# A gathered retrieval beside a dense one: table rows fetched in pairs, the dot products split over two engines, and one more block's top-k inside the dense stage

## The chip, the cores and the metric

One Trainium2 chip, one core. The metric is the time of one execution on the device in microseconds (us). The engines are TensorE (PE: matmuls; PEld: its weight loads), VectorE (DVE), ScalarE (ACT), GpSimd (POOL) and SyncE (SP), and 16 DMA engines move the data. Each engine takes its instructions in the order of its own queue.

## The reference

One decoder layer on 1024 tokens of width 1024: a modulated norm, gMLP heads and an S5 state-space part side by side, an output projection with a residual, then a retrieval over 16384 experts, and a final norm. The retrieval is what matters here:

```
q = (t @ w_q).reshape(tb, HEADS, 2, DKEY // 2)              # t: a block of 128 tokens
s = einsum('thcd,hckd->thck', q, keys)                      # 8 heads, 2 halves, 128 keys
top_s, top_i = top_k(s, 16)                                 # per half
cand = all sums of one entry of each half;  best_s, pos = top_k(cand, 16)
idx = the experts of pos;  g = softmax(best_s)
act = gelu(einsum('thkd,td->thk', u_tab[idx], t))           # first table
return einsum('thk,thkd->td', g * act, v_tab[idx])          # second table
```

So each token uses 128 expert slots (8 heads of 16), each with a row of 1024 fp32 in the first table (`peer_u`) and one in the second (`peer_v`).

## The kernel before

The tokens form 8 blocks of 128. A **lead** of some 920 us computes everything up to the scores, along a written-out plan (`CFG["plan"]`): each item, such as `r6`, which is `route(6)`, the top-k of block 6, has a due time and a number of steps, and the items' steps are put in order by those times. A planner of the framework then sets each engine's queue order from that program order and its own estimate of when operands are ready. On the chip the order of a queue is fixed.

**Dense stage, blocks 0 to 4.** Their 640 tokens meet all 16384 experts, in 128 tiles of 128 experts. For tile `i`, `stage1(i)` (L918 to L933) multiplies the tile of the first table, split into a high and a low part `uh`, `ul`, with the tokens, `Th` and `Tl`, into PSUM banks `pa`: 48 matmuls (L930), and a gelu on ScalarE (L932) frees the bank. `load_u(i + 2)` brings the tile through one buffer `ur` (ScalarE casts the high part, L906; VectorE subtracts, L907), `load_v(i)` the tile of the second table through one buffer `vr` (L914, L915). `weigh` multiplies two tiles' results by the routing weights of the group (`Gt`, L949) and splits them into `wh` and `wl` (L951, L953). After every fourth tile `stage2` multiplies the group's weights with its `v` tiles: 120 matmuls `pd` (L977) and `res` (L968); VectorE adds what `pd` gives to `acc` (L985). The first five tiles' `stage1` lies in the lead.

**Gathered blocks 5 to 7.** `side_work()` is a generator that the dense loop advances: `pull(6)` after each tile. It first runs `route(b)` for the blocks from `NDB + early` on, which is block 7 alone; its 28 steps work on VectorE, and the scores come from DRAM by SyncE's queue, two heads at a time (`scr`, L761). Then the pool `kp` of the top-k is closed and the pool `rp` opened. For each block there are 128 steps on the first table: GpSimd gathers a row per token (L872), and one fused VectorE instruction multiplies it with `hn` and sums (L875) into a column of `act`. Then 128 steps on the second table: a gather (L883) and a multiply-add into `gacc` (L888). Rows live in a ring of six. At a block's end `load_x1` (on GpSimd's queue, kept in program order) brings the tokens' residual, and `finish` (L829 to L845) multiplies by `gt2`, adds, norms and writes out. The two constant rows for `finish`, `gt2` and `g_final`, are loaded once by `final_rows`, into two tiles of their own.

**The end.** After the loop `pull(10 ** 9)` draws what is left of the generator; then the last `stage2` loads five blocks' residuals on GpSimd's queue (L851) and calls `finish` for the five dense blocks. For them VectorE multiplies and adds straight from PSUM banks (L835, L836), which is what frees those banks. The loop:

```
    for i in range(NE):
        if i >= L: run(stage1(i))
        if L <= i + 2 < NE: load_u(i + 2)
        ...
        if i % 2: weigh(i // 2)
        if i % QG: load_v(i)
        pull(cfg["per"])
        if i % QG == 0:
            ...
    pull(10 ** 9)
    stage2(NGR - 1)
```

Of the kernel before, what the change touches and what calls it, by code (L numbers as in the profile page):

```python
# [21 lines left out]
P = 128  # L22
# [14 lines left out]
NS = NH * TOPK  # L37
NE = 128
QG = 4
FMAX = 3.0e38  # L40
CFG = dict(xo=[2, 3, 4, 0, 1], gt=3, ss=7, hs=2, b1=6, nw=6, raw=1, ngb=3, rows=6, lead=5, per=6, dv=[6, 9, 9, 2, 99], early=2,
           hp=600, eo=(2, 4), em={2: 'pppxx', 4: 'Xpp'}, seg=4, plan=dict(
    op0=(-238.2, 44.5), sb0=(-21, 248.8), m5=(-490.1, 3.4), r0=(234.1, 82.1), op1=(132.1, 27.3), op2=(292.7, 7.7),
    sb1=(310, 10.8), op3=(364.9, 36.8), r1=(301.9, 79), s0=(261.5, 137.5), sb2=(303.2, 61.7), zv=(372.6, 16.7),
# [23 lines left out]
def rows(ap, n=P):  # L68
    return bass.AP(tensor=ap.tensor, offset=ap.offset, ap=[[0, n]] + [list(d) for d in ap.ap])
# [27 lines left out]
def tile_hybrid_layer(ctx: ExitStack, tc: tile.TileContext, a, out, cfg=CFG):  # L97
# [752 lines left out]
    def load_x1(b, x1):  # L850
        tc.keep_in_program_order(nc.gpsimd.dma_start(x1, x1_d[b * P:(b + 1) * P, :]))  # L851
        return x1

    def final_rows(pool):
        for n, src in enumerate((gt2_d, rows(a["g_final"]))):
            fin.append(pool.tile([P, D], F32, name=f"fin{n}", bufs=1))
            nc.scalar.dma_start(fin[n], src)

    def side_work():
        for b in range(NDB + cfg["early"], NB):  # L860
            yield from route(b)
        kp.release()
        rp = rq[0] = ctx.enter_context(tc.tile_pool(name="rp", bufs=cfg["rows"], side="left"))
        final_rows(rp)
        for n in range(NGB):
            ix, gw = tops[NDB + n]
            hn = rp.tile([P, D], F32, tag="hn", name=f"hn{n}", bufs=1)
            nc.scalar.dma_start(hn, h2_d[n * P:(n + 1) * P, :])
            act = rp.tile([P, NS], F32, tag="act", name=f"act{n}", bufs=1)
            for s in range(NS):  # L870
                row = rp.tile([P, D], F32, tag="row", name=f"ru{n}_{s}")
                G.indirect_dma_start(out=row, out_offset=None, in_=a["peer_u"],  # L872
                                     in_offset=bass.IndirectOffsetOnAxis(ap=ix[:, s:s + 1], axis=0))
                junk = rp.tile([P, D], BF16, tag="junk", name=f"jk{n}_{s}", bufs=1)
                V.tensor_tensor_reduce(out=junk, in0=row, in1=hn, scale=1.0, scalar=0.0, op0=ALU.mult,  # L875
                                       op1=ALU.add, accum_out=act[:, s:s + 1])
                yield
            A.activation(act, act, AF.Gelu_apprx_tanh)
            V.tensor_mul(act, act, gw)
            ac = rp.tile([P, D], F32, tag="hn", name=f"gacc{n}", bufs=1)  # L880
            for s in range(NS):
                row = rp.tile([P, D], F32, tag="row", name=f"rv{n}_{s}")
                G.indirect_dma_start(out=row, out_offset=None, in_=a["peer_v"],  # L883
                                     in_offset=bass.IndirectOffsetOnAxis(ap=ix[:, s:s + 1], axis=0))
                if s == 0:
                    V.tensor_scalar(ac, row, act[:, 0:1], None, op0=ALU.mult)
                else:
                    V.scalar_tensor_tensor(ac, row, act[:, s:s + 1], ac, op0=ALU.mult, op1=ALU.add)  # L888
                yield
            x1 = load_x1(NDB + n, rp.tile([P, D], F32, tag="row", name=f"xf{n}"))  # L890
            finish(NDB + n, x1, [(slice(0, D), ac)], rp, *fin)

    side = side_work()
# [1 line left out]
    def pull(n):  # L895
        for _ in range(n):
            if next(side, 0) == 0:
                return
# [196 lines left out]
    for i in range(NE):  # L1095
# [9 lines left out]
            weigh(i // 2)  # L1105
        if i % QG:
            load_v(i)
        pull(cfg["per"])
        if i % QG == 0:
            if i >= max(L, 1):  # L1110
                stage2(i // QG - 1)
# [352 lines left out]
```

## Time and profile before

| | |
|---|---|
| time, median of 3 runs | 2660.49 us (2659.53 to 2662.55) |
| profiled execution | 2662.87 us, span of its instructions 2661.1 us |
| TensorE busy | 95% |
| VectorE busy | 86% |
| ScalarE busy | 34% |
| GpSimd busy | 41% |
| DMA, mean | 272 GB/s |

The span runs from the first to the last instruction of the profiled execution; 1.8 us of its time lie around it. Times in the rows below are microseconds from the span's start unless marked ns. An engine's share is taken over the whole span, which has a lead, a dense stage and a tail with different limits. Matmuls are pipelined, so a busy TensorE is not one at its peak rate.

### The profile page before, as it was taken

The page shows a single profiled execution, that of the slowest core. Times are in us where ns is not written, and L with a number is a line of the kernel's source. Part 1 is how long each engine was busy: PE and PEld are TensorE (multiplying, and loading weights), DVE is VectorE, ACT ScalarE, POOL GpSimd, SP SyncE. Part 2 cuts the span into 40 slices and gives each one's busy share as a digit, 9 for nine tenths or more (in the row PEclk, how much of TensorE's full clock was granted, in tenths as well). Part 3 has the DMA queues.
Part 4 walks back from the last instruction along what each step waited for, and adds up shares of the span by engine and source line. Part 5 has one row for each costly group of instructions (what it writes and reads, how often), then busy time and mean ns, then how long its engine had stood idle before and what let it go on. Part 6 is the DMA issues. An engine that isn't in the chain of part 4 may idle for free.

```text
span 2661.1 us, 38843 instructions
## 1 busy us (share of the span) xinstructions
PE 2539.9 (95%) x14119; PEld 2174.0 (82%) x14119; DVE 2295.9 (86%) x4791; ACT 900.7 (34%) x1547; POOL 1093.2 (41%) x842
## 2 busy tenths in 40 slices
PE   6999999999877999999999999999999999999996
PEld 3557676678666899999999999999999999999995
DVE  7884699869899798888998888888898888888898
ACT  2211246568968322222222222222222222222221
POOL 0001000000000066566666566666666566666662
PEclk9996999999987999999999999999999999999998
DMA  9555333444646699999999999999999999999995
GB/s 366 103 151 177 109 117 105 128 135 135 172 120 191 217 359 344 344 331 336 333 349 348 317 351 336 348 345 332 334 337 345 344 337 336 340 344 345 324 322 188
DMA packets 301184, 724.74 MB, mean 272 GB/s; under 512 B 42384, under 2 KB 133008, under 8 KB 300576
## 3 DMA queue, kind: packets, MB, share of 16 engines
q0 software_dynamic: 112832, 411.09, 42.8%
q1 hardware_dynamic: 165600, 254.48, 28.8%
q10 hardware_dynamic: 22560, 56.69, 6.0%
q8 instruction: 111, 1.82, 0.3%
q14 instruction: 81, 0.66, 0.1%
HBM read 658.60 MB, written 62.39 MB: 271 GB/s over the span
## 4 chain that ended last, share of the span: by engine, by line
PE 72%; DVE 15%; ACT 5%; issue 3%; DMA 2%; POOL 1%; ACTq 0%; DVEq 0%; POOLq 0%
PE pa L930 31%; PE res L968 15%; PE pd L977 15%; ACT b L687 3%; PE pq L725 2%; PE po L626 2%; PE pzs L360 2%; POOL rv L883 1%; DMA scr<-sc_d 1%; DVE a L679 1%; PE pgs L689 1%; DVE ixs L1350 1%; ACT GS L692 1%; DVE ixs L1353 1%; PE py L567 1%
## 5 line engine op out<-in xcount | busy, mean ns | idle before, releaser
L872 POOL DMA_INDIRECT ru<-in_peer_u_dram,ix x384 | 531.7, 1385 | 974.6 <-issue 715.1
L930 PE MATMUL pa<-Th,u 128*128 128x320 f32 x4096 | 909.7, 310 | 3.6 <-DVE u L907 3.2
L930 PEld LDWEIGHTS pa<-Th,u 128*128 128x128 f32 x4096 | 688.2, 188 | 5.6 <-DVE u L907 3.7
L883 POOL DMA_INDIRECT rv<-in_peer_v_dram,ix x384 | 541.4, 1410 | 309.4 <-DVE gacc L888 230.6
L930 PE MATMUL pa<-Tl,u 128*128 128x320 f32 x2048 | 634.1, 310 | 0.0
L888 DVE SCALAR_TENSOR_TENSOR gacc<-rv,act,gacc 128x1024 f32<-128x1024 f32 x381 | 488.7, 1283 | 22.0 <-DMA rv<-in_peer_v_dram,ix 17.2
L875 DVE CUSTOM_DVE_ANT_0 jk<-ru,hn 128x1024 bf16<-128x1024 f32 x384 | 469.1, 1222 | 32.4 <-DMA ru<-in_peer_u_dram,ix 21.4
L977 PE MATMUL pd<-v,wh 128*128 128x512 f32 x1280 | 399.1, 391 | 11.7 <-DVE x L836 10.6
L968 PE MATMUL res<-v,wh 128*128 128x512 f32 x1280 | 398.5, 389 | 0.0
L930 PEld LDWEIGHTS pa<-Tl,u 128*128 128x128 f32 x2048 | 385.7, 188 | 1.2
L906 ACT CAST u<-ur 128x1024 fp32r<-128x1024 f32 x128 | 134.2, 1049 | 624.9 <-PE res L968 511.7
L932 ACT ACTIVATE w<-pa 128x320 f32<-128x320 f32 x256 | 112.0, 438 | 541.6 <-PE pa L930 531.9
L977 PEld LDWEIGHTS pd<-v,wh 128*128 128x128 f32 x1280 | 239.9, 188 | 60.6 <-DVE x L836 11.0
L968 PEld LDWEIGHTS res<-v,wh 128*128 128x128 f32 x1280 | 240.2, 188 | 49.8
L687 ACT ACTIVATE b<-hot,gT 128x128 f32<-128x128 f16 x520 | 235.1, 553 | 61.0 <-PE pgs L689 36.6
L968 PE MATMUL res<-v,wl 128*128 128x512 f32 x640 | 248.6, 389 | 0.0
L977 PE MATMUL pd<-v,wl 128*128 128x512 f32 x640 | 248.1, 390 | 0.0
L689 PE MATMUL pgs<-a,b 128*128 128x128 f32 x1280 | 191.1, 302 | 44.2 <-DVE a L679 18.8
L689 PEld LDWEIGHTS pgs<-a,b 128*128 128x128 f32 x1280 | 172.2, 209 | 66.5 <-ACT b L687 34.8
L985 DVE TENSOR_TENSOR acc<-acc,pd 128x512 f32<-128x512 f32 x150 | 102.3, 686 | 95.1 <-PE pd L977 91.2
L907 DVE TENSOR_TENSOR u<-ur,u 128x1024 fp32r<-128x1024 f32 x128 | 156.3, 1221 | 14.0 <-ACT u L906 12.6
L914 ACT CAST v<-vr 128x1024 fp32r<-128x1024 f32 x128 | 134.1, 1048 | 91.2 <-DMA vr<-in_peer_v_dram 91.2
(348 smaller groups left out, 2910.9 us busy)
## 6 DMA issues: line engine op xcount, KB each, us to landing
vr<-in_peer_v_dram SPq DMA_DIRECT2D x128, 512.0 KB
ur<-in_peer_ut_dram SPq DMA_DIRECT2D x128, 512.0 KB
G_d<-GS SPq DMA_DIRECT2D x40, 1024.0 KB
Gt<-G_d ACTq DMA_DIRECT2D x64, 640.0 KB
wada<-in_w_ada_dram SPq DMA_DIRECT2D x17, 1024.0 KB
wo<-in_w_out_dram SPq DMA_DIRECT2D x8, 1024.0 KB
ru<-in_peer_u_dram,ix POOLq DMA_INDIRECT x384
rv<-in_peer_v_dram,ix POOLq DMA_INDIRECT x384
```

Of the source, the lines that this page charges most:

```text
L687: A.activation(b1[:, n], hot[:, :, o + n], AF.Copy, scale=gT[:, s1 + o + n:s1 + o + n + 1])
L689: T.matmul(pg[:, o // 4, (o % 4) * P:(o % 4 + 1) * P], b1[:, o % 2], a1[:, o % 4], start=True, stop=True)
L872: G.indirect_dma_start(out=row, out_offset=None, in_=a["peer_u"], in_offset=bass.IndirectOffsetOnAxis(ap=ix[:, s:s + 1], axis=0))
L875: V.tensor_tensor_reduce(out=junk, in0=row, in1=hn, scale=1.0, scalar=0.0, op0=ALU.mult, op1=ALU.add, accum_out=act[:, s:s + 1])
L883: G.indirect_dma_start(out=row, out_offset=None, in_=a["peer_v"], in_offset=bass.IndirectOffsetOnAxis(ap=ix[:, s:s + 1], axis=0))
L888: V.scalar_tensor_tensor(ac, row, act[:, s:s + 1], ac, op0=ALU.mult, op1=ALU.add)
L906: A.copy(u[:, 0], ur)
L907: V.tensor_tensor(u[:, 1], ur, u[:, 0].bitcast(F32), op=ALU.subtract)
L914: A.copy(v[:, 0], vr)
L930: T.matmul(pa[:, :NN], l[:, k, :], r[:, k, ns], start=(k == 0 and m == 0), stop=(k == KD - 1 and m == 2))
L968: T.matmul(res[tb][n], l[:, ts], r[:, n * 512:(n + 1) * 512], start=(g == 0 and q == 0 and m == 0), stop=(g == NGR - 1 and q == QG - 1 and ...
L977: T.matmul(po, l[:, ts], r[:, n * 512:(n + 1) * 512], start=(q == 0 and m == 0), stop=(q == QG - 1 and m == 2))
```

## The change

Three things change. The dense stage's `side_work` starts with block 6 (`early` 2 to 1), and a route there yields at every third of its steps. The first-table phase fetches two rows a slot, multiplies both with `hn` in one VectorE instruction in place, and one pair later sums each product with a ScalarE copy that has an accumulator. The loop draws 6.4 steps a tile on average instead of 6. With it go a ring of four slots of two rows, second-table rows in pairs whose products stay as they were, and `final_rows` at each block's end into a slot of the ring. The plan's table of due times is not touched.

```diff
-CFG = dict(... rows=6, lead=5, per=6, dv=[6, 9, 9, 2, 99], early=2,
+CFG = dict(... rows=4, lead=5, per=6.4, dv=[6, 9, 9, 2, 99], early=1,
...
-    def final_rows(pool):
-        for n, src in enumerate((gt2_d, rows(a["g_final"]))):
-            fin.append(pool.tile([P, D], F32, name=f"fin{n}", bufs=1))
-            nc.scalar.dma_start(fin[n], src)
+    def final_rows(pool, n):
+        f = pool.tile([P, GP, D], F32, tag="row", name=f"fin{n}")
+        for e, src in enumerate((gt2_d, rows(a["g_final"]))):
+            nc.scalar.dma_start(f[:, e], src)
+        fin[:] = [f[:, 0], f[:, 1]]
 
     def side_work():
         for b in range(NDB + cfg["early"], NB):
-            yield from route(b)
+            for k, _ in enumerate(route(b)):
+                if k % 3 == 0:
+                    yield
         kp.release()
...
-            for s in range(NS):
-                row = rp.tile([P, D], F32, tag="row", name=f"ru{n}_{s}")
-                G.indirect_dma_start(out=row, ...)
-                junk = rp.tile([P, D], BF16, tag="junk", name=f"jk{n}_{s}", bufs=1)
-                V.tensor_tensor_reduce(out=junk, in0=row, in1=hn, scale=1.0, scalar=0.0, op0=ALU.mult,
-                                       op1=ALU.add, accum_out=act[:, s:s + 1])
+            def fetch(src, s0, name):
+                row = rp.tile([P, GP, D], F32, tag="row", name=f"{name}{n}_{s0}")
+                for e in range(GP):
+                    G.indirect_dma_start(out=row[:, e], ...)
+                return row
+
+            def sums(s, row):
+                for e in range(GP):
+                    A.activation(junk, row[:, e], AF.Copy, accum_out=act[:, s + e:s + e + 1])
+
+            prev = None
+            for s in range(0, NS, GP):
+                row = fetch("peer_u", s, "ru")
+                V.tensor_mul(row, row, bcast(hn, 1, GP))
                 yield
+                if prev:
+                    sums(*prev)
+                prev = s, row
+                yield
+            sums(*prev)
...
-            x1 = load_x1(NDB + n, rp.tile([P, D], F32, tag="row", name=f"xf{n}"))
+            for s in range(0, NS, GP):
+                row = fetch("peer_v", s, "rv")
+                for e in range(GP):
...
+                    yield
+            final_rows(rp, n)
+            x1 = load_x1(NDB + n, rp.tile([P, GP, D], F32, tag="row", name=f"xf{n}")[:, 0])
...
-        pull(cfg["per"])
+        pull(int((i + 1) * cfg["per"]) - int(i * cfg["per"]))
```

## Rows read from the trace of the kernel before

**Rows 1.** The page: busy time, share of the span and instructions of each engine, and the clock that TensorE was granted, in tenths, over 40 equal slices.

```profile
PE 2539.9 (95%) x14119; PEld 2174.0 (82%) x14119; DVE 2295.9 (86%) x4791; ACT 900.7 (34%) x1547; POOL 1093.2 (41%) x842
PEclk9996999999987999999999999999999999999998
```

**Rows 2.** Busy time of each engine in stretches of the span. Columns: from and to, length, busy us and instructions of PE, PEld, DVE, ACT and POOL, granted clock, DMA share, GB/s.

```profile
848.00:884.00 36.00, 33.25 (x226) 32.44 (x224) 31.39 (x150) 16.57 (x30) 0.00 (x0) 0.97 0.60 187
884.00:923.00 39.00, 37.05 (x167) 31.93 (x168) 32.38 (x115) 15.97 (x20) 3.02 (x4) 0.92 0.51 168
923.00:1089.00 166.00, 166.00 (x937) 151.91 (x936) 143.16 (x206) 42.22 (x55) 104.31 (x77) 1.00 0.95 352
1255.00:2584.00 1329.00, 1329.00 (x7490) 1216.24 (x7489) 1180.28 (x1347) 334.86 (x439) 846.42 (x603) 1.00 0.93 338
2605.00:2661.00 56.00, 29.58 (x122) 23.71 (x120) 48.59 (x128) 9.77 (x24) 11.98 (x12) 0.80 0.48 172
```

**Rows 3.** The chain of waits that ended last, three of its steps: start, length, engine, group and count.

```profile
978.12 28.16 PE pa L930 x192
...
1033.50 28.16 PE pa L930 x192
...
2473.38 28.16 PE pa L930 x192
```

**Rows 4.** The start of the dense stage, single entries of the timeline of SyncE, VectorE and TensorE: start, length, engine and line, operation, count, and in brackets the idle time before it with what ended it.

```profile
848.60 0.33 SPq L761 DMA_DIRECT2D scr<-sc_d  x1
886.17 16.91 SPq L912 DMA_DIRECT2D vr<-in_peer_v_dram  x3
...
884.94 1.21 DVE L915 TENSOR_TENSOR v<-vr,v 128x1024 fp32r<-128x1024 f32 x1
907.43 1.23 DVE L915 TENSOR_TENSOR v<-vr,v 128x1024 fp32r<-128x1024 f32 x1 [0.71 <-ACT v L914]
917.82 0.23 DVE L771 CAST ix<-fi 128x128 int32<-128x128 f32 x1
930.03 1.23 DVE L875 CUSTOM_DVE_ANT_0 jk<-ru,hn 128x1024 bf16<-128x1024 f32 x1 [5.84 <-DMA hn<-h_d]
...
884.87 0.90 PE L930 MATMUL pa<-Th,u 128*128 128x320 f32 x2 [2.74 <-DVE u L907]
907.45 0.50 PE L977 MATMUL pd<-v,wh 128*128 128x512 f32 x1 [1.08 <-ACT v L914]
```

**Rows 5.** The same columns as in rows 2, for two short stretches of the start; the clock is the first of the last three numbers.

```profile
884.00:890.00 6.00, 5.13 (x19) 5.13 (x20) 6.00 (x29) 0.00 (x0) 0.00 (x0) 0.50 0.93 300
891.00:900.00 9.00, 9.00 (x49) 7.96 (x48) 8.24 (x49) 4.45 (x6) 0.00 (x0) 1.00 0.25 79
```

**Rows 6.** VectorE alone in 848 to 918: all its instructions, and then those that touch the scores `scr`, the candidates `ca` and the masks `mk`, in this order. Columns: stretch, length, VectorE busy us and instructions, clock, DMA share, GB/s.

```profile
848.00:918.00 70.00, 62.56 (x262) 0.94 0.55 175
848.00:918.00 70.00, 20.91 (x128) 0.94 0.55 175
848.00:918.00 70.00, 8.38 (x73) 0.94 0.55 175
848.00:918.00 70.00, 12.78 (x20) 0.94 0.55 175
```

**Rows 7.** Groups of instructions of the gathered part over the whole span: line, engine, operation, count, busy us and mean ns of one, idle time before them and what ended most of it.

```profile
L872 POOL DMA_INDIRECT ru<-in_peer_u_dram,ix x384 | 531.7, 1385 | 974.6 <-issue 715.1 <-DVE act L875 230.5 <-DVE w L949 16.1
L888 DVE SCALAR_TENSOR_TENSOR gacc<-rv,act,gacc 128x1024 f32<-128x1024 f32 x381 | 488.7, 1283 | 22.0 <-DMA rv<-in_peer_v_dram,ix 17.2
L875 DVE CUSTOM_DVE_ANT_0 jk<-ru,hn 128x1024 bf16<-128x1024 f32 x384 | 469.1, 1222 | 32.4 <-DMA ru<-in_peer_u_dram,ix 21.4 <-DMA hn<-h_d 5.8
L875 DVE DVE_READ_ACCUMULATOR2_ANT act<- 128x1 f32 x384 | 31.6, 82 | 0.0
```

**Rows 8.** The same view, groups whose shape or operation is near to what the change adds: products and differences of two operands on VectorE, a function with an accumulator and its read on ScalarE.

```profile
L907 DVE TENSOR_TENSOR u<-ur,u 128x1024 fp32r<-128x1024 f32 x128 | 156.3, 1221 | 14.0 <-ACT u L906 12.6 <-issue 1.1
L953 DVE TENSOR_TENSOR wl<-w,wh 128x1280 fp32r<-128x1280 f32 x64 | 95.0, 1484 | 1.0 <-ACT wh L951 1.0
L837 ACT ACTIVATE sqf<-xf 128x1024 bf16<-128x1024 f32 x3 | 3.2, 1055 | 26.3 <-DVE xf L836 26.3
L837 ACT ACTIVATION_READ_ACCUMULATOR sqf<-xf 128x1 f32 x3 | 0.6, 188 | 0.0
```

**Rows 9.** VectorE alone, as in rows 6, just after the gathers began.

```profile
930.00:955.00 25.00, 24.62 (x35) 1.00 0.99 375
```

**Rows 10.** The first and the last gather, and the end of the span: entries of the timeline of GpSimd, VectorE and TensorE as in rows 4, and one short stretch with the columns of rows 2.

```profile
919.07 1.02 POOL L872 DMA_INDIRECT ru<-in_peer_u_dram,ix  x1 [661.59 <-issue]
2615.14 1.86 POOL L883 DMA_INDIRECT rv<-in_peer_v_dram,ix  x1 [0.66 <-DVE gacc L888]
2617.55 2.69 POOL L851 DMA_DIRECT2D x<-x_d  x5
...
2625.16 0.69 DVE L1007 TENSOR_TENSOR x<-x,acc 128x512 f32<-128x512 f32 x1 [3.68 <-DMA x<-x_d]
2656.53 1.42 DVE L844 SCALAR_TENSOR_TENSOR x<-x,rf,fin 128x512 f32<-128x512 f32 x2
...
2637.62 1.22 PE L977 MATMUL pd<-v,wh 128*128 128x512 f32 x2 [10.58 <-DVE x L836]
2638.00:2641.00 3.00, 3.00 (x8) 2.33 (x8) 3.00 (x7) 0.35 (x1) 0.00 (x0) 0.50 0.00 0
```

More of the change, by code (lines that the diff above doesn't have):

```diff
@@ L39 @@
 QG = 4
+GP = 2
 FMAX = 3.0e38
-CFG = dict(xo=[2, 3, 4, 0, 1], gt=3, ss=7, hs=2, b1=6, nw=6, raw=1, ngb=3, rows=6, lead=5, per=6, dv=[6, 9, 9, 2, 99], early=2,
+CFG = dict(xo=[2, 3, 4, 0, 1], gt=3, ss=7, hs=2, b1=6, nw=6, raw=1, ngb=3, rows=4, lead=5, per=6.4, dv=[6, 9, 9, 2, 99], early=1,
            hp=600, eo=(2, 4), em={2: 'pppxx', 4: 'Xpp'}, seg=4, plan=dict(
@@ L852, in load_x1 @@
         return x1
-    def final_rows(pool):
-        for n, src in enumerate((gt2_d, rows(a["g_final"]))):
-            fin.append(pool.tile([P, D], F32, name=f"fin{n}", bufs=1))
-            nc.scalar.dma_start(fin[n], src)
+    def final_rows(pool, n):
[3 more added lines that the diff above has]
+        fin[:] = [f[:, 0], f[:, 1]]
     def side_work():
         for b in range(NDB + cfg["early"], NB):
-            yield from route(b)
+            for k, _ in enumerate(route(b)):
+                if k % 3 == 0:
+                    yield
         kp.release()
         rp = rq[0] = ctx.enter_context(tc.tile_pool(name="rp", bufs=cfg["rows"], side="left"))
-        final_rows(rp)
         for n in range(NGB):
@@ L869, in side_work @@
             act = rp.tile([P, NS], F32, tag="act", name=f"act{n}", bufs=1)
-            for s in range(NS):
-                row = rp.tile([P, D], F32, tag="row", name=f"ru{n}_{s}")
-                G.indirect_dma_start(out=row, out_offset=None, in_=a["peer_u"],
-                                     in_offset=bass.IndirectOffsetOnAxis(ap=ix[:, s:s + 1], axis=0))
-                junk = rp.tile([P, D], BF16, tag="junk", name=f"jk{n}_{s}", bufs=1)
-                V.tensor_tensor_reduce(out=junk, in0=row, in1=hn, scale=1.0, scalar=0.0, op0=ALU.mult,
-                                       op1=ALU.add, accum_out=act[:, s:s + 1])
-                yield
+            junk = rp.tile([P, D], BF16, tag="junk", name=f"jk{n}", bufs=1)
+            def fetch(src, s0, name):
+                row = rp.tile([P, GP, D], F32, tag="row", name=f"{name}{n}_{s0}")
+                for e in range(GP):
+                    G.indirect_dma_start(out=row[:, e], out_offset=None, in_=a[src],
+                                         in_offset=bass.IndirectOffsetOnAxis(ap=ix[:, s0 + e:s0 + e + 1], axis=0))
+                return row
[6 more added lines that the diff above has]
+                V.tensor_mul(row, row, bcast(hn, 1, GP))
+                yield
+                if prev:
[3 more added lines that the diff above has]
+            sums(*prev)
             A.activation(act, act, AF.Gelu_apprx_tanh)
@@ L880, in side_work @@
             ac = rp.tile([P, D], F32, tag="hn", name=f"gacc{n}", bufs=1)
[L881 to L889, printed above, removed]
-            x1 = load_x1(NDB + n, rp.tile([P, D], F32, tag="row", name=f"xf{n}"))
+            for s in range(0, NS, GP):
+                row = fetch("peer_v", s, "rv")
+                for e in range(GP):
+                    w = act[:, s + e:s + e + 1]
+                    if s + e == 0:
+                        V.tensor_scalar(ac, row[:, e], w, None, op0=ALU.mult)
+                    else:
+                        V.scalar_tensor_tensor(ac, row[:, e], w, ac, op0=ALU.mult, op1=ALU.add)
+                    yield
+            final_rows(rp, n)
+            x1 = load_x1(NDB + n, rp.tile([P, GP, D], F32, tag="row", name=f"xf{n}")[:, 0])
             finish(NDB + n, x1, [(slice(0, D), ac)], rp, *fin)
```

## The prediction

> **What bounds the kernel now.** I read the page's shares first, then the span cut into stages, then the chain of waits, and then the two ends of the dense stage instruction by instruction. TensorE is busy 95% of the span [rows 1]. The stages show that this average hides three regimes [rows 2]. From 923 to 2605 TensorE never stops, and the chain of waits consists of its matmuls alone: one run of 192 `pa` matmuls starts every 55.38 us (978.12, 1033.50, and so on to 2473.38), 28.16 us for four tiles of experts and 27.22 us for the group's second stage [rows 3]. Nothing that the change does to VectorE, ScalarE or the gathers can shorten that stretch; it can only lengthen it. What can get shorter or longer is its two ends. At the start (848 to 923) TensorE has small gaps, 2.74 us at 884.87 behind a split of an expert tile on VectorE and 1.08 us at 907.45 behind a `v` tile [rows 4]. At the end (2605 to 2661) it is busy 29.58 of 56 us at a mean clock of 0.80 [rows 2]; that end hangs on the gathers, as shown below.
>
> The gathers run beside the dense stage: 768 steps from 919.07 to 2615.14, 2.208 us each or 25.1 per period of 55.38 us [rows 10]. VectorE is 86 to 89% busy there, the DMA engines 93 to 95%, ScalarE 25% [rows 2]. So the gathers' pace is set by VectorE and the DMA engines together, and it matters only for when the last one is done.
>
> **Part 1: the top-k that is added.** The edit `early=1` makes the dense stage run `route(6)` and `route(7)`. But the written-out plan still lists `r6`, and nothing drops it, so the lead is not relieved: block 6's top-k is done twice, and the first result is replaced unread. The price is one more top-k where block 7's runs now. In 848 to 918 VectorE spent on it 20.91 us on the scores, 8.38 on the candidates and 12.78 on the masks, together 42.1 of its 62.56 busy us; 7.4 us were idle [rows 6]. The gathers wait for the last index list (917.82, first issue 919.07 [rows 4, 10]), because the pool that they use opens only when the top-k's pool closes. So they start later by 42.1 − 7.4 = 35 us.
>
> What TensorE loses is the question. Before the tile `v3` and the second `weigh` come, the old program has put 18 of the one route's 28 steps into its queue order; the new one has taken 19 pulls of up to 3 steps, 53 of 56. Group 0's second stage needs all four `v` tiles, and they pass one buffer in turn: split, then the next load, which waits at the head of SyncE's queue (16.91 us for three issues at 886.17), with the `u` loads behind it; their splits are at 884.94 and 907.43 [rows 4]. Below, the cost is nothing, if the planner slips the splits into the gaps between dependent top-k instructions, as the 884.94 split stands among them now. Above, it is the whole 35 us plus a clock loss. I take a middle near what the rows show for a dense operation between top-k instructions: `v2` waits 2.74 us, like the `u` split now, and `v3` one pair of score heads, 20.91 / 4 = 5.2 us: 8 us. The clock: after the 2.74 us gap, 884 to 890 ran at 0.50, and 891 to 900 at 1.00 [rows 5]; one more such stretch of 6 us does half its work, 3 us. Start: **+11** (0 to 38).
>
> **Part 2: the first table in pairs.** Removed are 384 fused products of 1.222 us and 384 accumulator reads of 0.082 us on VectorE [rows 7]. Added are 192 products of 128x2048, which the trace does not have. From above they cost two of 128x1024, 2 × 1.221 = 2.44 us; from the step 1024 to 1280 (1.221 to 1.484) the slope is 1.03 ns an element, so 1.221 + 1.05 = 2.27 us [rows 8], which I take. VectorE saves 2 × 1.304 − 2.27 = 0.34 us a pair, 65 us in all (33 by the upper bound), none of it on TensorE's path. ScalarE gets 384 copies with a sum; the nearest rows are a square of the same size, 1.055, and its read, 0.188: 1.243 us each [rows 8]. Its dense work is 334.86 of 1329 us, 3.49 a tile [rows 2]; with 6.3 rows a tile it reaches 3.49 + 7.8 = 11.3 of 13.85 us, 82%. The gelus that free TensorE's banks stand in that queue, but a tile's bank is wanted some 14 us later and a sum holds the queue 1.24 us, so I cost this at nothing; if several sums stacked up behind a late product, it would be a few us.
>
> The Trainium skill ("ScalarE: Activation LUTs", section "Rules for kernel authors") speaks against this part: products and additions belong on VectorE, not on ScalarE. The rows do not settle it for the sums: 1.243 us there against nothing extra in the fused form, but on an engine that idles 75%. By the page 384 sums were better left; by the rows the move frees 65 us of the engine that paces the gathers. Its way of going wrong is in the third rival.
>
> **Part 3: pairs in the second table, the ring, the final rows.** The products into `gacc` stay (1.283 us each [rows 7]); slots come free in twos. The ring holds four pairs in place of six rows plus two rows of constants, the same bytes. The constants are now loaded at each block's end, on ScalarE's queue, into a pair slot. Such an issue waits until VectorE has freed the slot, and the gelus stand behind it. Bounds: nothing, or three times the 5.84 us that the first product waits for its operand now [rows 4], 17; I take 1 us each, **+3**.
>
> **Part 4: 6.4 steps a tile.** It moves the gathers ahead in program order: 796 steps were drawn by 6 a tile, so 28 remained after the loop, ahead of the last second stage; now 788 are drawn by tile 123. It sets order, not pace.
>
> **The tail.** The last gather is issued at 2615.14; the `x` rows of the dense blocks stand behind it on GpSimd's queue (2617.55) and the first use of them on VectorE is at 2625.16. TensorE has begun the last second stage at 2605, needs 27.2 us, and stops for 10.58 us until VectorE frees a bank (2637.62); then it runs at 0.50 [rows 10]. Without that it would end at 2605 + 27.2 = 2632, not at 2645. After it, the end comes 16 us later now; with the `x` rows early, only the last block's products, scale and write-out remain, some 12. Tail: 2661 − 2644 = **−17** (bounds 0 and −20), if the `x` rows are there in time, with the last gather at or before about 2614 on the new clock. Dense work is 14 us later, the gathers start 35 later, so 1696 us of gathering must shrink by 36; all of it in the first-table rows: 384 × 2.208 = 848 to 812, 26.2 rows a period. VectorE's saving of 4 us a period gives room for three rows; the DMA engines, at 94%, for six in a hundred, 26.6. That 930 to 955 moved 375 GB/s, against 338 later [rows 2, 9], speaks for it. I take it as reached, narrowly.
>
> **Sum.** +11 + 3 − 17 = −3. The profiled execution took 2662.87 us, its span 2661.1 with 1.8 around it; 2659.9. The median of the runs shown is 2660.49, 2.4 below that execution, so **2657.5 us**. Differences under 0.2%, 5.3 us, count as the same here: about what a measurement of this kernel can tell from no change.
>
> **Rivals.**
> 1. *The start is hidden.* The splits fall into gaps, as 884.94 does; start 0 to 4, boundaries 0 to 3, tail −17 to −20: 2640 to 2651. Against it: VectorE has 7 us idle for 42 of work.
> 2. *The other side: the second top-k stands ahead of group 0's operands.* The orderer puts all 53 steps before `v3` and the second `weigh`; start +38, with boundaries +3 and tail −17 this is +24: 2684, and 2670 to 2693 for most of it. It decides from a start cost of about 20 us on. For it: program order. Against it: in 848 to 884, with block 6's and block 7's top-k interleaved, TensorE was still busy 33.25 of 36 us [rows 2].
> 3. *The gathers do not get earlier.* Their pace stays at 25 a period, because the DMA engines are full, four pair slots turn slower than six rows, or ScalarE's sums come late and hold the slots (the rule above). Then the last gather is at 2615 + 35 = 2650, and the 46 us from it to the end follow unchanged: +35, 2695; with a part of the gain 2672 to 2700. It decides below 25.8 rows a period, where all of the tail's gain is lost.
> 4. *The change is a move after all:* the first copy of block 6's top-k is not run or was what held the lead, so up to 35 us drop out ahead: about 2623.
>
> **Chances.** Forecast (2652 to 2665) 0.34; rival 1 0.17; rival 2 0.24; rival 3 0.20; rival 4 0.05. The forecast's own range straddles the 0.2%: of its 0.34, 0.08 faster, 0.20 same, 0.06 slower. Faster: 0.08 + 0.17 + 0.05 = 0.30. Same: 0.20. Slower: 0.06 + 0.24 + 0.20 = 0.50. The likeliest single case is the forecast, though slower as a whole is likelier. The range 2642 to 2692 takes the forecast, most of rivals 1 and 2 and some two thirds of rival 3, about 0.83.
>
> **What would show it.** Right: score instructions of block 6 a second time after 850; the last index list near 952; group 0's second stage ending some 11 us later than now; pair products of 2.2 to 2.4 us; ScalarE above 75% in the first-table phases and TensorE without gaps there; more than 26 rows a period; the `x` rows landed before the last second stage ends, and no stop of 10 us in it. Wrong: a gap of over 20 us before 960, gathers still issued after 2630, or `pa` runs further apart than 55.38 us.

## The result and the profile after

The changed kernel takes 2681.79 us in the median (2676.92 to 2683.66), the kernel before 2661.24 in the same comparison: a ratio of 1.008, 95% interval 1.0068 to 1.0092. It is slower by 20.5 us. The forecast was 2657.5, the same or a little faster; the range to 2692 holds the time, but the likeliest case fell on the wrong side. Line numbers of the changed kernel are up to 19 higher behind the edit: `pa` is L949, `pd` L996, `res` L987, a gather L878, the pair's product L889, its sums L884.

The page of the changed kernel, busy time of each engine, then the first two stretches of [rows 2], others of the dense stage and the tail; the last line is the kernel before from 923 to 2584 (length, PE, PEld, DVE, ACT, POOL busy, clock, DMA share, GB/s):

```profile
PE 2548.1 (95%) x14119; PEld 2175.7 (81%) x14119; DVE 2302.7 (86%) x4442; ACT 1317.7 (49%) x2318; POOL 1177.3 (44%) x842
848.00:884.00 36.00, 32.36 (x223) 31.43 (x222) 31.93 (x148) 15.01 (x26) 0.00 (x0) 1.00 0.66 201
884.00:923.00 39.00, 33.24 (x156) 26.82 (x155) 38.18 (x198) 14.28 (x18) 0.00 (x0) 1.00 0.47 152
923.00:960.00 37.00, 35.48 (x224) 33.65 (x223) 36.88 (x147) 17.07 (x22) 0.00 (x0) 1.00 0.43 136
1089.00:1255.00 166.00, 163.10 (x908) 148.86 (x907) 133.64 (x92) 120.05 (x202) 129.51 (x75) 0.98 0.92 328
923.00:2584.00 1661.00, 1652.39 (x9295) 1509.61 (x9294) 1441.46 (x1280) 833.92 (x1317) 1122.67 (x743) 1.00 0.92 336
2620.00:2682.00 62.00, 33.44 (x133) 26.61 (x131) 57.56 (x136) 11.70 (x26) 14.80 (x16) 0.77 0.61 226
...
923.00:2584.00 1661.00, 1661.00 (x9360) 1520.05 (x9359) 1468.86 (x1739) 418.73 (x548) 1050.83 (x754) 1.00 0.93 340
```

TensorE is no longer gapless in the dense stage: it is busy 1652.39 of the 1661 us from 923 to 2584, where the kernel before has all 1661. VectorE is full from 884 to 960, where the second top-k runs, and GpSimd issues nothing before 960. The tail looks as before, only later. The first and the last gather, the `x` rows behind it, the stop in the last second stage, and the first matmuls of `stage1` for tile 9 and for the loop's last three tiles, from the timeline; the last two lines are those two of the kernel before:

```profile
967.09 1.02 POOL L878 DMA_INDIRECT ru<-in_peer_u_dram,ix  x1 [711.70 <-issue]
2635.67 1.02 POOL L878 DMA_INDIRECT rv<-in_peer_v_dram,ix  x1 [0.30 <-DMA vr<-in_peer_v_dram]
2640.39 2.63 POOL L852 DMA_DIRECT2D x<-x_d  x5
...
2654.66 1.22 PE L996 MATMUL pd<-v,wh 128*128 128x512 f32 x2 [7.01 <-DVE x L837]
...
981.74 0.30 PE L949 MATMUL pa<-Th,u 128*128 128x320 f32 x1
2600.50 0.30 PE L949 MATMUL pa<-Th,u 128*128 128x320 f32 x1
...
977.96 0.30 PE L930 MATMUL pa<-Th,u 128*128 128x320 f32 x1
2583.98 0.30 PE L930 MATMUL pa<-Th,u 128*128 128x320 f32 x1
```

From the last gather to the end of the span it is 2682.0 − 2635.7 = 46.3 us; before, 2661.1 − 2615.1 = 46.0 [rows 10]. So the whole loss is that of the last gather, +20.5 us, and that is a sum of four parts. The issue times of the first and the last gather of each of the six phases give them: the start is 48.0 later (967.1 against 919.1); the three first-table phases take 854.6 instead of 837.3 us, +17.3; the three second-table phases 786.2 instead of 844.6, −58.4; the gaps between phases 27.8 instead of 14.1, +13.7. Together +20.6, the 20.5 within rounding. TensorE lost less and did not decide: its second group begins 3.8 us later (981.74 against 977.96), its last run 16.5 us later (2600.5 against 2584.0).

The gathers' groups over the span (mean ns of one, idle before and releasers), and what VectorE and ScalarE do on the first table:

```profile
L878 POOL DMA_INDIRECT ru<-in_peer_u_dram,ix x384 | 643.6, 1676 | 935.2 <-issue 798.7 <-ACT jk L884 77.8 <-DVE xf L845 20.2
L878 POOL DMA_INDIRECT rv<-in_peer_v_dram,ix x384 | 513.5, 1337 | 277.1 <-DVE gacc L906 189.9 <-issue 74.5 <-ACT jk L884 8.1
L889 DVE TENSOR_TENSOR ru<-ru,hn 128x2048 f32<-128x2048 f32 x192 | 438.5, 2288 | 107.5 <-DMA ru<-in_peer_u_dram,ix 105.0 <-issue 1.4 <-DVE w L968 0.8
L884 ACT ACTIVATE jk<-ru 128x1024 bf16<-128x1024 f32 x384 | 405.5, 1056 | 223.5 <-issue 142.8 <-DVE ru L889 53.9 <-ACT jk L884 11.6
L884 ACT ACTIVATION_READ_ACCUMULATOR jk<-ru 128x1 f32 x384 | 72.1, 188 | 0.0
```

VectorE saved what was worked out, but it then waits 105 us for rows (21.4 before [rows 7]), and a first-table gather issue costs GpSimd 1.676 us, against 1.385. Idle time of VectorE with rows missing, and GpSimd waiting for ScalarE's sums, suggest that the slots come back too late, not that VectorE is short of time; e4, e5 and e7 below test it.

### The profile page after: what moved, and what is told of

Read it like the earlier page. It is cut to its first block, busy times and chain, and to the rows that moved or that the text cites. A ratio compares the mean times of both kernels' runs of the same rounds, so it can differ in the third digit from the quotient of the medians.

```text
span 2682.0 us, 39299 instructions
## 1 busy us (share of the span) xinstructions
PE 2548.1 (95%) x14119; PEld 2175.7 (81%) x14119; DVE 2302.7 (86%) x4442; ACT 1317.7 (49%) x2318; POOL 1177.3 (44%) x842
## 3 DMA queue, kind: packets, MB, share of 16 engines
q0 software_dynamic: 112832, 411.09, 42.1%
## 4 chain that ended last, share of the span: by engine, by line
PE 60%; DVE 21%; DMA 7%; ACT 5%; issue 3%; POOL 1%; ACTq 0%; DVEq 0%; POOLq 0%
PE pa L949 25%; PE pd L996 12%; PE res L987 12%; DMA ru<-in_peer_u_dram,ix 5%; ACT b L688 3%; DVE ru L889 2%; PE po L627 2%; DMA scr<-sc_d 2%; PE pq L726 2%; DVE ixs L1369 1%; PE pgs L690 1%; DVE ixs L1372 1%; DVE a L680 1%; PE pzs L361 1%; ACT GS L693 1%
## 5 line engine op out<-in xcount | busy, mean ns | idle before, releaser
L878 POOL DMA_INDIRECT ru<-in_peer_u_dram,ix x384 | 643.6, 1676 | 935.2 <-issue 798.7
L949 PE MATMUL pa<-Th,u 128*128 128x320 f32 x4096 | 911.7, 310 | 4.9 <-DVE u L926 3.1
L949 PEld LDWEIGHTS pa<-Th,u 128*128 128x128 f32 x4096 | 688.9, 188 | 9.0 <-DVE u L926 3.6
L878 POOL DMA_INDIRECT rv<-in_peer_v_dram,ix x384 | 513.5, 1337 | 277.1 <-DVE gacc L906 189.9
L949 PE MATMUL pa<-Tl,u 128*128 128x320 f32 x2048 | 634.1, 310 | 0.0
L889 DVE TENSOR_TENSOR ru<-ru,hn 128x2048 f32<-128x2048 f32 x192 | 438.5, 2288 | 107.5 <-DMA ru<-in_peer_u_dram,ix 105.0
L884 ACT ACTIVATE jk<-ru 128x1024 bf16<-128x1024 f32 x384 | 405.5, 1056 | 223.5 <-issue 142.8
L996 PE MATMUL pd<-v,wh 128*128 128x512 f32 x1280 | 405.0, 392 | 14.1 <-DVE x L837 7.0
L987 PE MATMUL res<-v,wh 128*128 128x512 f32 x1280 | 401.5, 391 | 6.8 <-ACT wh L970 4.4
L949 PEld LDWEIGHTS pa<-Tl,u 128*128 128x128 f32 x2048 | 385.7, 188 | 1.5
L996 PEld LDWEIGHTS pd<-v,wh 128*128 128x128 f32 x1280 | 240.2, 189 | 65.5 <-DVE x L837 7.4
L987 PEld LDWEIGHTS res<-v,wh 128*128 128x128 f32 x1280 | 239.8, 188 | 57.4 <-ACT wh L970 5.4
L987 PE MATMUL res<-v,wl 128*128 128x512 f32 x640 | 248.8, 390 | 1.4 <-DVE wl L972 1.4
L996 PE MATMUL pd<-v,wl 128*128 128x512 f32 x640 | 248.8, 391 | 0.3 <-DVE wl L972 0.3
```

What stands on the lines that cost most here:

```text
L878: G.indirect_dma_start(out=row[:, e], out_offset=None, in_=a[src], in_offset=bass.IndirectOffsetOnAxis(ap=ix[:, s0 + e:s0 + e + 1], axis=0))
L884: A.activation(junk, row[:, e], AF.Copy, accum_out=act[:, s + e:s + e + 1])
L889: V.tensor_mul(row, row, bcast(hn, 1, GP))
L949: T.matmul(pa[:, :NN], l[:, k, :], r[:, k, ns], start=(k == 0 and m == 0), stop=(k == KD - 1 and m == 2))
L987: T.matmul(res[tb][n], l[:, ts], r[:, n * 512:(n + 1) * 512], start=(g == 0 and q == 0 and m == 0), stop=(g == NGR - 1 and q == QG - 1 and ...
L996: T.matmul(po, l[:, ts], r[:, n * 512:(n + 1) * 512], start=(q == 0 and m == 0), stop=(q == QG - 1 and m == 2))
```

## Experiments

All paces are rows of a phase per 55.38 us, the group's period of [rows 3], from the issue times of its first and last gather.

| kernel | first gather | first table, blocks 5, 6, 7 | second table, blocks 5, 6, 7 | last gather | time, us |
|---|---|---|---|---|---|
| before | 919 | 25.5, 25.0, 25.1 | 25.1, 25.0, 24.8 | 2615 | 2660 |
| changed | 967 | 25.1, 24.6, 24.4 | 27.2, 26.5, 26.8 | 2636 | 2681.8 |
| e1, `r6` out of the plan | 966 | 25.3, 24.6, 24.4 | 27.4, 27.3, 26.9 | 2623 | 2677.9 |
| e2, `early=2` | 918 | 25.1, 24.6, 24.3 | 27.3, 26.7, 27.3 | 2585 | 2658.3 |
| e3, before with `early=1` | 970 | 26.0, 24.9, 25.0 | 25.0, 25.2, 26.3 | 2650 | 2690.3 |
| e4, fused sums | 971 | 29.3, 27.1, 27.1 | 27.6, 28.0, 28.4 | 2510 | 2658.8 |
| e5, fused and `early=2` | 920 | 28.3, 27.6, 27.2 | 28.4, 28.5, 27.9 | 2454 | 2654.9 |
| e9, product split | 968 | 27.0, 26.3, 26.1 | 28.0, 27.6, 27.8 | 2550 | 2661.7 |
| e7, three pairs | 969 | 21.6, 21.3, 21.4 | 25.7, 25.5, 27.9 | 2788 | 2837.5 |
| e10, split, three pairs | 968 | 25.0, 23.6, 24.1 | 25.4, 25.5, 26.9 | 2680 | 2727.0 |

**The added top-k, three ways.** Taken out of the plan (e1), taken out of the dense stage (e2), and put alone into the kernel before (e3).

```diff
 e1: CFG plan of the changed kernel
-... r5=(916.4, 58.6), r6=(989.9, 124.6), ld=(776, 675.7),
+... r5=(916.4, 58.6), ld=(776, 675.7),
 e2: changed kernel
-per=6.4, dv=[6, 9, 9, 2, 99], early=1
+per=6.4, dv=[6, 9, 9, 2, 99], early=2
 e3: kernel before
-per=6, dv=[6, 9, 9, 2, 99], early=2
+per=6, dv=[6, 9, 9, 2, 99], early=1
```

> The changed kernel with r6 taken out of the plan, so that block 6's top-k is done once, in the dense stage. Theory A (the last gather sets the end, 46 us behind it): the dense stage's own start and the gathers move earlier together by what the lead gives back, between nothing and the 35 us of VectorE time, and nothing else changes: 2647 to 2682 us, the last gather still about 1715 us after the first dense-stage instructions of block 7's top-k. Theory B (TensorE's stalls at the start set the loss, the gathers are cover): the stalls after 884 stay at about 10 us in all, and the time is the same as the changed kernel's within 5 us unless the lead itself gets shorter.

> The changed kernel with early=2: the pairs, the ring and 6.4 steps stay, block 6's top-k is done in the lead alone. Theory A: the gathers start near 919 again, 48 us earlier than in the changed kernel (967), their last issue is near 2588, before TensorE's last first-stage matmul, and the tail loses its 10 us stop: 2645 to 2652 us. Theory C (the sums on ScalarE slow the first-table phases and TensorE with them, and that is the loss): the gathers gain only what the second-table phases give and TensorE keeps its stalls: 2665 us or more.

> The kernel before with early=1 alone: only the doubled top-k, no pairs, six rows, 6 steps a tile. Theory A: the gathers start some 45 us later at the old pace, the last one is near 2660 and the end 46 us behind it: 2700 to 2710 us, slower than the changed kernel. Theory B: TensorE's stalls at the start alone, 10 to 17 us: 2671 to 2678 us.

Measured: e1 2677.86 us, ratio to before 1.0065 (1.0047 to 1.0083). e2 2658.28, 0.9995 (0.9985 to 1.0005), no change that could be told. e3 2690.27, 1.0111 (1.0094 to 1.0128).

e2 and e3 bear theory A out in direction: with the start back at 918, the loss of the changed kernel is gone (e2); with the doubled top-k alone, the kernel before loses 30 us (e3), and its tail stops for 29.47 us. e1 does not tell A from B, for its time lies in A's range and also within 5 us of the changed kernel's. The tail of e3:

```profile
2650.25 1.01 POOL L883 DMA_INDIRECT rv<-in_peer_v_dram,ix  x1 [0.30 <-issue]
...
2660.86 1.22 PE L977 MATMUL pd<-v,wh 128*128 128x512 f32 x2 [29.47 <-DVE x L836]
```

Theory A's numbers were off in e2 and e3. In e3 the last gather is at 2650, not 2660 (its last phase ran at 26.3, from 2590 on at 29.9, while the dense stage's loads ran out: the last one is issued at 2601.9), and it is 40.5 us from there to the end. In e2 the last gather is early enough, 2585, and the stop in the tail is gone, but 2645 to 2652 was not reached: TensorE is busy 1654.38 of the 1661 us from 923 to 2584 and its last matmul starts at 2640.20, some 8 us after what an undisturbed dense stage would give (2632). That is theory C's loss, in part.

e1 shows that a true move would have been worth some 4 us, and the intervals of e1 and the changed kernel overlap: the lead's last matmuls do end some 8 us earlier (the run of `pa` behind them begins at 850.7, against 859.0 in the changed kernel), but TensorE then stops 8.1 us at 861 and the gathers start at 966, as in the changed kernel. Its last gather is 12.8 us earlier and its span only 7.3 shorter, for TensorE, with its last run of `pa` at 2602.7, is by then close behind.

**The first table with the fused sums on the same ring (e4).**

```diff
-                V.tensor_mul(row, row, bcast(hn, 1, GP))
-                yield
-                if prev:
-                    sums(*prev)
-                prev = s, row
-                yield
-            sums(*prev)
+                for e in range(GP):
+                    V.tensor_tensor_reduce(out=junk, in0=row[:, e], in1=hn, ..., accum_out=act[:, s + e:s + e + 1])
+                    yield
```

> The changed kernel with the fused VectorE product and sum in the first-table phase, on the same ring of four pairs; the doubled top-k stays. Theory A with the slot's hold as the pace of the first table (product 2.3 us, then 2.4 us of sums on ScalarE before the slot is free): the hold shrinks, the first-table pace rises from 24.5 to 25.1 rows a period of 55.38 us to about 26.5, as in the second-table phases, the last gather comes 45 to 50 us earlier, near 2588, and the tail's stop goes: 2650 to 2660 us. If VectorE's or the DMA engines' load is what paces the first table, the pace stays at 25 and the time at 2675 to 2685 us.

Measured: 2658.83 us, 0.9993 (0.9983 to 1.0003). The first-table pace rises from 24.4 to 25.1 rows to 27.1 or more, though VectorE's work per pair grows from 2.29 to 2.61 us: the load of VectorE did not pace the first table, nor did the DMA engines at the old 25. The last gather is at 2510, 125 us earlier, two and a half times what was expected: 95 us of it come from the first table, twice what was expected there, and 32 from the second-table phases, which the edit does not touch; why those became faster too is not shown. The time fell by only 23 us, for behind the gathers stands TensorE: its last matmul starts at 2645.30, and the end comes 14.6 us after that one has ended. That is the limit the forecast's tail aimed at.

**The ring, the product's length, the draw (e7, e9, e8, e10).**

```diff
 e7: -rows=4, lead=5     +rows=3, lead=5
 e8: -per=6.4            +per=6
 e9: -                V.tensor_mul(row, row, bcast(hn, 1, GP))
     +                for e in range(GP):
     +                    V.tensor_mul(row[:, e], row[:, e], hn)
 e10: e9 with rows=3
```

> The changed kernel with a ring of three pairs instead of four. If the slots' round trip paces the gathers (17.4 us from a slot's issue to its next in the first-table phases, about 16.5 in the second), three quarters of the slots give some 20 and 22 rows a period, about 1950 us of gathering instead of 1669, and 2900 us or more in all, the tail included. If VectorE and the DMA engines pace them, 24.5 and 27 rows stay: 2680 to 2690 us.

> The changed kernel with 6 steps a tile instead of 6.4. If the number only orders the queues and the slots pace the gathers, the last gather stays within 5 us of 2636 and the time at 2676 to 2687 us. If the higher draw puts more of the top-k ahead of the dense operands at the start, TensorE's gaps between 890 and 950 shrink; with the end set by the gathers even that leaves the time there.

> The changed kernel with two products of 128x1024 in place of the one of 128x2048; the sums stay on ScalarE. One GpSimd gather issue takes 1.68 us there in the first-table phases, against 1.39 before and 1.38 in the run with the fused form. If the long VectorE instruction is what slows the issues, they fall to 1.4 us and the pace rises above 25 rows a period: 2665 to 2678 us. If it is the kind of instruction or the sums, they stay above 1.6 us, the product takes 2.44 instead of 2.29 us, and the pace stays at 24 to 24.5: 2682 to 2692 us.

> Two products of 128x1024 in place of one of 128x2048, on a ring of three pairs, where the slots' round trip is surely the limit: with the one long product it gave 21.4 rows a period, 15.5 us from a slot's issue to its next. Two causes are still open for what the split gained on four pairs. If it is the hold (after the second row has landed: one product of 1.2 and one sum of 1.2 instead of 2.3 and 2.4 us, 2.3 us less a turn, and 0.5 us less in the two issues), the round trip falls to about 12.9 us, 25.5 rows a period, and the time to some 2690 us. If it is GpSimd's issues alone (1.56 to 1.4 us, 0.3 to 0.5 us a turn), 22 rows a period and about 2800 us.

Measured: e7 2837.5 us and e10 2727.0 (one run each); e8 2681.89, 1.008 (1.0065 to 1.0096), the changed kernel's own time, so the draw of 6.4 does nothing that can be seen in the time (the profiled execution, the slowest of its four at 2690.8 us, has its last gather at 2642, 6 us later where at most 5 had been expected); e9 2661.73, 1.0006 (0.9997 to 1.0016), 20 us faster than the changed kernel for nothing but two instructions in place of one.

e7 says that the ring is what paces: three quarters of the slots, and the first table falls from 24.7 to 21.4 rows, the second, in blocks 5 and 6, from 27.2 and 26.5 to 25.7 and 25.5 (block 7's, 27.9, runs on past the loads of the dense stage). It did not fall in full proportion, and the expected 2900 us was too much: with fewer rows in flight the rest of the round trip gets shorter. With six rows in pairs the second table is back near the 25 that six single rows gave before; most of its gain in the changed kernel came from eight rows instead of six.

e9 was expected, in its better case, at 2665 to 2678; it went beyond. GpSimd's mean issue falls as well. The groups of first-table gathers, changed kernel (whole span, above: 1676 ns) against e9 and e4, and then, within block 6's phase alone, e7 and e10:

```profile
L878 POOL DMA_INDIRECT ru<-in_peer_u_dram,ix x384 | 549.0, 1430 | 971.3 <-issue 793.4 <-ACT jk L884 138.3 <-DVE xf L845 17.8
L878 POOL DMA_INDIRECT ru<-in_peer_u_dram,ix x384 | 529.9, 1380 | 953.1 <-issue 794.2 <-DVE act L890 122.9 <-DVE xf L845 16.8
...
L878 POOL DMA_INDIRECT ru<-in_peer_u_dram,ix x127 | 191.9, 1511 | 144.5 <-ACT jk L884 89.0 <-issue 23.9 <-DMA ru<-in_peer_u_dram,ix 8.7
L878 POOL DMA_INDIRECT ru<-in_peer_u_dram,ix x127 | 177.8, 1400 | 123.4 <-ACT jk L884 91.7 <-issue 21.9 <-DMA out_dram<-xf 4.0
```

e10 lies between its two expectations, nearer to that of the hold. The four traces say more: in the timelines of GpSimd, VectorE and ScalarE each slot's two issues can be matched, in order, with its product and its sums. Means of the first-table phases of blocks 5 to 7, without the first eight and the last few pairs of each, in us:

| kernel | a slot's turn | its two issues | end of the second issue to end of the last sum | from there to the slot's next issue |
|---|---|---|---|---|
| changed, four pairs | 17.8 | 3.7 | 12.6 | 1.4 |
| e9, split, four pairs | 16.5 | 3.2 | 12.7 | 0.6 |
| e7, three pairs | 15.5 | 3.5 | 11.5 | 0.5 |
| e10, split, three pairs | 13.6 | 3.1 | 10.0 | 0.5 |

On three pairs most of what the split gains, 1.5 of 1.9 us, is the hold: a long product can start only when both rows are there, and the first sum only when it has ended, while the split one has done the first row before the second lands. The two issues give 0.4. On four pairs, where the split won 20 us, the stretch that holds the rows is no shorter (part of it can be rows that have landed and wait for VectorE); the 1.3 us are 0.5 in the two issues and 0.8 in the time for which a free slot waits for its next issue. So there the gain shows at GpSimd: at 1.676 us an issue and the 0.30 us that stand between two of them, a pair takes 3.95 us of GpSimd's queue in the changed kernel, of the 4.45 us that a pair has at four pairs in 17.8 us.

**What is left without the losses (e5), and its draw (e11), and a true move on top of the fused form (e12).** e5 is e4 with `early=2`; e11 is e5 with 5.5 steps a tile; e12 is e4 with `r6` out of the plan, as in e1.

> The changed kernel with the fused VectorE product and sum and with early=2: what is left of the change is the ring of four pairs, the constants loaded per block and 6.4 steps. If the changed kernel's losses are the doubled top-k and the sums on ScalarE, and its gain the ring: the gathers start near 918, keep 27 rows a period or more, and end before 2470; TensorE's last first-stage matmul is back near 2606, its last matmul near 2634 and the end 15 us later: 2647 to 2653 us, faster than both kernels. If the loss of 8 us that TensorE shows in the run with early=2 comes from the block ends or the faster gathers' transfers instead of the sums: 2655 to 2660 us.

> The fastest kernel so far (fused product and sum, early=2, ring of four pairs) with 5.5 steps a tile instead of 6.4. Its gathers end 150 us before the dense stage, so they could be drawn later. If the 4 us that TensorE loses between 980 and 2590 there come from gather instructions that stand ahead of dense ones in VectorE's order, drawing them later gives some of it back: 2650 to 2654 us. If the queue order depends on readiness alone, nothing changes: 2653 to 2657 us, the last gather again near 2454.

> The fused product and sum on the ring of four pairs, and block 6's top-k truly moved: out of the plan, into the dense stage. The gathers start near 966 and end near 2505, with time to spare, so only TensorE decides. Theory M (the lead's relief is worth what it took off VectorE): the first dense tiles start some 10 us earlier, as they did in the run without r6 in the plan (850.7 against 859 to 862), and stay earlier: 2642 to 2650 us. Theory N (the relief is lost again before the second stage of group 0, behind one 8 us gap at 861 and the top-k in front of the operands): the second group starts near 984 to 987, and the time is 2655 to 2661 us.

Measured: e5 2654.89 us, 0.9978 (0.9969 to 0.9987), faster than both kernels by 5 and 27 us. e11 2654.09, 0.9976 (0.9967 to 0.9985), the same as e5, with the last gather again at 2454: 5.5 steps a tile change nothing that can be seen. e12 2659.98, 0.9996 (0.9986 to 1.0006): theory N, the lead's relief is lost behind a gap of 8.1 us at 864, and the second group begins at 986.7, no earlier than in e4 (986.5). e5's stretches, TensorE first, show where it stands:

```profile
923.00:2584.00 1661.00, 1658.61 (x9341) 1515.92 (x9340) 1494.33 (x1771) 421.89 (x550) 1038.18 (x769) 1.00 0.92 347
2500.00:2610.00 110.00, 110.00 (x621) 100.60 (x620) 42.01 (x42) 25.39 (x34) 1.61 (x3) 1.00 0.27 89
2610.00:2653.00 43.00, 28.14 (x127) 23.10 (x125) 26.94 (x97) 8.83 (x22) 1.05 (x2) 0.88 0.24 86
...
2637.75 0.39 PE L993 MATMUL pd<-v,wl 128*128 128x512 f32 x1
```

The gathers have ended at 2454, and the DMA engines fall to 27% after 2500; the last matmul ends at 2638.1 without a stop, and the end comes 14.8 us later. e5 was expected at 2647 to 2653; its last run of `pa` still begins 5.7 us later than in the kernel before (2589.64), where e2's begins 8.1 later. No wait of more than 1.3 us is left in its dense stage, and where these small gaps come from was not settled. e5 also says what paced the kernel before: it keeps that kernel's fused product and its top-k, the draw is without effect (e8, e11), and with a ring of eight rows instead of six its first table runs at 27.2 to 28.3 rows, not 25, with the DMA engines at 0.96 to 0.97.

## Why the prediction was wrong, step by step

**The doubling of the top-k** was right, and no lead time was saved. Its price was misread: VectorE's work from 848 to 966 is 43.13 us on the scores and 18.27 on the candidates, twice what [rows 6] have, but 20.49 on the masks, against 12.78. Of those 12.78 us 4.55 lie before 878 and end the lead's own top-k of block 6; one top-k's masks take 8.22. So one top-k is 37.5 us on these three, not 42.1. The changed kernel, and then the masks of the kernel before:

```profile
848.00:966.00 118.00, 112.78 (x501) 1.00 0.51 159
848.00:966.00 118.00, 43.13 (x256) 1.00 0.51 159
848.00:966.00 118.00, 18.27 (x146) 1.00 0.51 159
848.00:966.00 118.00, 20.49 (x31) 1.00 0.51 159
...
848.00:878.00 30.00, 4.55 (x8) 0.97 0.71 219
900.00:918.00 18.00, 8.22 (x12) 1.00 0.44 147
```

**The gathers' start** was a term of the wrong size: +35 forecast, +48 measured. Scores, candidates and masks grew by 39.8 us (81.9 less 42.1). The rest was left out of 42.1 − 7.4: VectorE did 10.4 us more of other work in the longer stretch, dense work and the rest of the second top-k (30.9 us against 20.5), and of the idle time only 2.2 us were used (5.2 us stay idle, of 7.4). 39.8 + 10.4 − 2.2 = 48.

**TensorE's start**: +11 forecast, +3.8 measured at the second group. The waits for the `v` tiles are there, but small (2.07, 1.31 and 1.54 us around 905), and the planner did slip their splits between top-k instructions. The clock term was not: after a gap of 2.69 us that ends at 883.25 the clock is 1.00 from 883 to 890, where [rows 5] had shown 0.50 after 2.74. That is one execution; e9 and e4, with the same doubled top-k, show 0.72 from 883 to 889 after a gap of 2.71 us and 0.50 from 886 to 892 after 2.44, and their second groups begin at 982.7 and 986.5. All of these are below the 20 us from which rival 2 was to decide; it is out, though its 2684 us is the time nearest to the measured one, by chance.

**The sums on ScalarE** were priced rightly by their records (1.056 + 0.188 us against 1.055 + 0.188 [rows 8]; the two overlap, and ScalarE is busy 71% of block 6's first-table phase, not 82%), and wrongly put at nothing. From the second group to the last run of `pa` TensorE fell another 16.5 − 3.8 = 12.7 us behind. Its waits from 985 to 2600 sum to 7.1 us; most are for the casts and gelus behind the sums in ScalarE's queue. Below them one case: a sum waits 5.69 us for a late product, the casts stand behind it, and TensorE waits for the second of them.

```profile
PE res L987 <- ACT wh L970: 3.0, 3, 1.5
PE res L987 <- DVE wl L972: 1.4, 1, 1.4
PE pd L996 <- ACT wh L970: 1.3, 1, 1.3
PE pa L949 <- ACT w L951: 1.1, 1, 1.1
...
1112.46 1.06 ACT L884 ACTIVATE jk<-ru 128x1024 bf16<-128x1024 f32 x1 [5.69 <-DVE ru L889]
1113.51 1.03 ACT L925 CAST u<-ur 128x1024 fp32r<-128x1024 f32 x1
1114.45 1.25 ACT L970 CAST wh<-w 128x1280 fp32r<-128x1280 f32 x1
1115.76 0.73 PE L987 MATMUL res<-v,wh 128*128 128x512 f32 x2 [1.49 <-ACT wh L970]
```

Behind this wait and one of 1.41 us that follows it the clock is 0.51 from 1120 to 1124; the 0.98 from 1089 to 1255 is worth some 3 us, and some 2 of the 12.7 are not accounted for. The other runs put a size on it: with `early=2` TensorE is busy 1654.38 of 1661 us from 923 to 2584 with the pair's product and the sums on ScalarE (e2), and 1658.61 with the fused form (e5). e9 shows what this term alone would have left of the forecast's gain: its gathers end at 2550, its last second stage has no stop, its sums are on ScalarE, and it takes 2661.7 us.

**The first-table pace** is the step that failed and turned the sign. It was taken to reach 26.2 rows because VectorE would have time; it was 25.1 to 24.4, and the three phases took 854.6 us, not the 812 of the forecast. What failed was the first sentence on the gathers: that VectorE and the DMA engines together set their pace. A slot's way from issue to issue sets it, within what these two allow: fewer slots slow it (e7), more slots speed up the form of before (e5), and more work on VectorE does not slow it (e4). The new form lengthens that way. Both rows must land, then come 2.29 us of product and the sums; and the long product makes the issues beside it longer, 1.676 us against 1.385, a term that the prediction did not have and that weighs most on four pairs. The product's length is the larger cause: split in two, with the sums still on ScalarE, the pace is 26.1 to 27.0 (e9); with the sums fused it is 27.1 to 29.3 (e4). In both the time returns to that of before, even with the top-k doubled. I had written a part of the mechanism down, as rival 3 (slots held by late sums), and gave it 0.20. Its 2695 us came down to 2682 only because the second table's unforeseen gain outweighed the later start, the slower first table and the longer block ends; that the range to 2692 holds the time is such a cancelling of misses, not a sign that the sum was right.

**The second table and the ring** were costed at nothing and brought 58 us: eight rows in flight instead of six gave 26.5 to 27.2 rows a period, most of it by e7. **The block ends** cost 13.7 us more in the gathers' chain, not at TensorE's gelus as I had put them: some 10 us stand between each second-table phase and the next first-table one (4.7 and 3.7 before), in which GpSimd waits for the finish of the block (`DVE xf`).

**The tail** was right as a mechanism and too large as a number: −17 with everything early. In e5 the stop is gone, and 14.8 us, not 12, remain after the last matmul: an undisturbed 2632.3 + 14.8 would be 2647, −14 (an estimate).

The Trainium skill, in "ScalarE: Activation LUTs", section "Rules for kernel authors", had advised against sums on ScalarE, because VectorE is faster per element, in bf16. In fp32 no row here shows that: a sum takes 1.056 us on ScalarE, VectorE's fused product and sum 1.222. The fastest kernels here keep the sums on VectorE all the same. What the runs show for it is that the casts TensorE waits for stand behind the sums and that the first-table pace is higher without them; in the time it is little: 2661.73 us with them on ScalarE (e9), 2658.83 with them fused (e4).

## What to carry to other kernels

A stream that is gathered through a few slots has the pace of a slot's round trip, its issues included. So price a change to its consumer by how long it holds a slot after the last row has landed, and by what it does to the engine that issues, not by how much engine time it frees. Batching two rows into one instruction makes each wait for both and passes nothing on until both are done, and here it also held up the gather issues beside it: two short instructions were worth 20 us over one long one that was cheaper by 0.15 us a pair. And when an edit moves work, check that the old place lets go of it: the doubled top-k alone cost the kernel before 30 us.

## What the runs showed of the hardware

GpSimd's issue of a gather takes 0.94 us by itself, and longer when a VectorE instruction with two operands in SBUF is already running: then it ends some 0.8 us after that instruction, where 0.94 us would have ended sooner. In block 6's first-table phase of the changed kernel 59 issues met a running product and took over 1 us; all of them end 0.80 to 0.86 us after it. From the changed kernel, a first-table stretch of VectorE and GpSimd:

```profile
1609.79 2.29 DVE L889 TENSOR_TENSOR ru<-ru,hn 128x2048 f32<-128x2048 f32 x1 [1.51 <-DMA ru<-in_peer_u_dram,ix]
1613.59 2.29 DVE L889 TENSOR_TENSOR ru<-ru,hn 128x2048 f32<-128x2048 f32 x1 [0.78 <-DVE w L968]
...
1610.22 2.67 POOL L878 DMA_INDIRECT ru<-in_peer_u_dram,ix  x1 [0.62 <-ACT jk L884]
1613.19 0.94 POOL L878 DMA_INDIRECT ru<-in_peer_u_dram,ix  x1 [0.30 <-issue]
```

The product from 1609.79 runs to 1612.08; the issue that began at 1610.22 ends at 1612.89. The next issue began before the next product and took 0.94. In block 6's first-table phase the longest issue is 3.04 us with the long product, and 1.98 in the kernel before, whose products take 1.22 us; issues that begin while an addition runs that reads one operand from PSUM (`acc`) take 0.94 to 0.95 in both. The Trainium skill ("SBUF — State Buffer", section "SBUF: two separate sides") has the rule: VectorE and GpSimd share a pair of ports as an exclusive lock, which whichever starts first holds for its whole instruction, a VectorE instruction with two SBUF inputs too when the GpSimd one reads SBUF (a gather here reads its indices from `ix` there). These rows agree, and they add that a longer VectorE instruction makes the wait longer: 112 us more of GpSimd's time over 384 issues. On four pairs that is where the split product's gain shows, on three pairs it is the smaller part; how much of the 20.5 us it is by itself stays open.
